# A hybrid encoder block in 3 x fp32r products on one core: rooms, ties and early weights in the input projection; keys, last-used tiles and sums of w_out in the tail

## The chip, the core and the metric

The kernel runs on one core of a Trainium2 chip. The core has a matrix engine (TensorE, PE in the profile), a vector engine (VectorE, DVE), a scalar engine (ScalarE, ACT), a general engine (GpSimd, POOL) and a queue that issues transfers (SyncE, SP). Each works through its own list of instructions in order; semaphores make one wait for another. The metric is the device time of one execution in microseconds (us), and lower is better.

## The reference

For x of 2048 tokens by 1024 channels, all in fp32:

```python
h = rms_norm(x, norm_pre_g)
u_a, z_a, q, k, v, o, z_b, gates, g_a, g_b = split(h @ w_in)          # 9 x 1024 columns and 16 gates
pooled = multiscale_pool(u_a)                                         # windows 2, 4, 8, 16, mean minus token
y_a = (pooled @ pool_mix_w (per group)) * pool_scale * silu(z_a)
q, k = silu(conv5([q, k]))                                            # centred, per channel
h_fwd, h_bwd = mlstm(q, k, v, gates) in both directions               # 4 heads of 256, chunks of 128
y_b = headwise_rms(h_fwd + h_bwd) * mlstm_norm_g * sigmoid(o) * silu(z_b)
merged = sigmoid(g_a + b0) * (y_a @ w_proj_pool) + sigmoid(g_b + b1) * (y_b @ w_proj_mlstm)
out = x + rms_norm(merged @ w_out, norm_post_g)
```

One direction of mlstm carries a 256 x 256 state per head from chunk to chunk. Per chunk it adds keys, weighted by exponentials of the gates, times values, and reads the state with the queries.

## The kernel before

Every large product is made of three fp32r matmuls: each operand is split into an upper half, a copy by ACT (L98), and a lower half, the difference, by DVE or POOL (L102); PE adds upper x upper, upper x lower and lower x upper (L110 to L112 or L1038 to L1040).

**Input projection (`phase1`, 0 to about 1494 us).** 36 pairs of column blocks are run over each half of 1024 tokens. `operands` loads x, computes the row norms (`sums`, with two dummy matmuls `busy` at L281) and makes the sums S1 to S4 (`combos`, L210 to L217) of Strassen's scheme. The first two pairs are plain products; the others take seven block products in place of eight (`strassen`). There ACT copies the first bank (p1, L463) and DVE adds it to later banks (u2 at L469, u3 at L474, output sums at L685 through `collect`); the next product into a bank waits until these have read it. In the first half `prep_w` makes each pair's weight sums T1 to T4 (L426) and `keep_w` stores them; in the second half `again_w` loads them. The gates' product leaves PSUM by an ACT copy (gsb, L671), for which the products of `fold` (fps, L373) wait; they multiply pool_mix_w into the weights of u. In the second half 16 pieces of w_proj_pool are fetched, split and stored again (`split_ahead`, one per pair from pair 12, 2 tiles from the pool `wt` of 3), and 32 masks for mlstm are built in tiles of the same pool (`masked`). Halo columns of neighbouring tokens are copied into each raw tile (L703, L765) before the convolution or the pooling.

**mLSTM (`mlstm`, to about 1830 us).** A backward pass over head 0's chunks 15 to 1 comes first: `back1` transposes keys (L1277, ACT copies them at L1280), `keys` weighs them (kw on ACT at L1239, upper half on DVE at L1240, lower half on POOL at L1241), `back2` updates the state. Then 64 steps, one per head and chunk, run the forward pass and the outputs (`front1` to `front3`, `finish`), with the next head's backward pass beside them. The pool `io` holds everything that rotates here, the gate tile gb and the normalised outputs too. The last yb store (L1470) is the last thing of this stage on SP.

**Projections and output.** `branch_a` multiplies y_a by w_proj_pool (paps, 8 groups of 128 columns x 4 blocks of 512 tokens) and by its gate (L1182), to about 1992 us; `branch_b` does y_b (pb), to about 2174; `output` is again Strassen's scheme, its weight sums of w_out made by `out_weights` (differences L1081) in part during `branch_b`, in part at its own start. The pools `w1` (8 tiles of 4 KB a partition), `w1b` (4) and `w2` (16) hold split weights. `w1` is opened at the start of the tail, and first written when weights of w_proj_pool are loaded during the steps (`turns`).

**What sets the order.** A scheduler places the instructions of each engine, by priority and by times that it simulates; `issue_after` ties one instruction behind another on the same engine only, and waits for data come besides. All DMAs are issued by SP in one list, so a transfer that has to wait for its data or for room holds up all that come after it. A tile's memory is free for the next tile when its last reader has ended; for a stored tile that is the landing of its store.

## Time and profile before

| | us |
|---|---|
| median of 3 runs | 2350.88 |
| lowest to highest | 2348.56 to 2352.04 |
| the profiled execution, own time | 2351.66 |
| its span in the trace | 2349.9 |
| PE busy | 2291.2 |
| DVE, POOL, ACT busy | 1428.9, 1182.4, 884.2 |
| mean granted clock of PE | 0.994 |
| moved by DMA | 550.80 MB |

The span is the time from the first to the last instruction of the profiled execution; the execution's own time lies 1.76 us above it. Times in the views count from the start of the span. In a row of a timeline stand the start, the length, the engine, the line, the operation, output and input, their shapes and, in brackets, how long the engine had been idle before it and what ended that. Lines (L...) are those of the kernel before.

### The profile page before, as it was taken

What the parts mean: (1) busy time and instruction counts of PE and PEld (TensorE: products, weight loads), DVE (VectorE), ACT (ScalarE), POOL (GpSimd) and SP (SyncE); (2) the same over time, 40 slices, a digit from 0 to 9 for tenths busy, and PEclk for the clock granted to TensorE, in tenths of its full rate; (3) what the DMA queues carried; (4) which work ended last, traced back from release to release, by engine and by line L of the source; (5) the groups of instructions that cost most, each with busy time, mean ns of one, the idle gap of its engine ahead of it and who ended that gap; (6) DMA issues with size and microseconds to landing.
All of it is one profiled execution on the core that took longest, in us unless ns stands there. A gap on an engine that the chain in (4) does not pass through costs nothing.

```text
span 2349.9 us, 32919 instructions
## 1 busy us (share of the span) xinstructions
PE 2291.2 (98%) x11545; PEld 1938.3 (82%) x11545; DVE 1428.9 (61%) x2383; ACT 884.2 (38%) x1795; POOL 1182.4 (50%) x917
## 2 busy tenths in 40 slices
PE   7999999999999999999989999999999899999998
PEld 5788888888888788888878788799998688999776
DVE  7765656767765565546656665489886322454765
ACT  5434332433334423322322233477676201111432
POOL 4655555666654534456555555355556200234865
PEclk9999999999999999999999999999999999999999
DMA  5567766766675366788888787777676745687753
GB/s 210 188 245 266 261 218 233 258 233 223 225 281 206 111 215 204 227 295 290 288 295 297 263 296 252 271 242 243 225 219 195 244 141 166 228 269 272 264 191 126
DMA packets 229238, 550.80 MB, mean 234 GB/s; under 512 B 23120, under 2 KB 70352, under 8 KB 229072
## 3 DMA queue, kind: packets, MB, share of 16 engines
q1 hardware_dynamic: 229072, 548.69, 68.2%
q8 instruction: 91, 1.49, 0.3%
q14 instruction: 75, 0.61, 0.1%
HBM read 335.22 MB, written 213.39 MB: 233 GB/s over the span
## 4 chain that ended last, share of the span: by engine, by line
PE 81%; DMA 7%; DVE 6%; issue 2%; POOL 2%; ACT 1%; SPq 1%; DVEq 0%; POOLq 0%; ACTq 0%
PE bankB L110 7%; PE bankB L112 7%; PE bankB L111 7%; PE bankA L110 5%; PE bankA L111 5%; PE bankA L112 5%; PE bankC L110 5%; PE bankC L111 5%; PE bankC L112 5%; PE num L1367 4%; PE pb L1040 3%; PE pb L1038 3%; PE pb L1039 3%; PE paps L1038 2%; PE paps L1039 2%; PE paps L1040 2%
## 5 line engine op out<-in xcount | busy, mean ns | idle before, releaser
L102 POOL TENSOR_TENSOR wB<-wraw,wB 128x512 fp32r<-128x512 f32 x224 | 338.0, 1513 | 302.1 <-ACT wB L98 214.5
L98 ACT ACTIVATE wB<-wraw 128x512 fp32r<-128x512 f32 x228 | 141.8, 625 | 271.8 <-PE bankB L112 133.7
L102 POOL TENSOR_TENSOR wT<-wt,wT 128x512 fp32r<-128x512 f32 x102 | 148.9, 1464 | 132.7 <-ACT wT L98 105.9
L718 DVE SCALAR_TENSOR_TENSOR acc<-raw,conv_w,acc 128x1026 f32<-128x1026 f32 (+1 forms) x96 | 152.2, 1597 | 10.5 <-ACT acc L713 9.7
L1040 PE MATMUL pb<-oxs,w_proj_mlstm 128*128 128x256 f32 x512 | 143.9, 281 | 0.0
L1039 PE MATMUL pb<-oxs,w_proj_mlstm 128*128 128x256 f32 x512 | 143.8, 281 | 0.0
L1038 PE MATMUL pb<-oxs,w_proj_mlstm 128*128 128x256 f32 x512 | 143.8, 281 | 0.0
L98 ACT ACTIVATE wT<-wt 128x512 fp32r<-128x512 f32 x136 | 85.2, 629 | 150.1 <-PE bankB L112 57.1
L1351 POOL TENSOR_TENSOR qs<-q,isc 128x256 f32<-128x256 f32 x120 | 89.8, 752 | 85.3 <-PE num L1367 53.9
L110 PE MATMUL bankB<-S3h,wT 128*128 128x512 f32 x272 | 106.7, 392 | 3.7 <-DVE u L469 3.7
L110 PE MATMUL bankB<-A22h,wT 128*128 128x512 f32 x272 | 106.3, 391 | 2.9 <-DVE u L474 2.9
L1038 PE MATMUL paps<-pys,w_proj_pool 128*128 128x512 f32 x256 | 102.0, 399 | 6.2 <-DMA w_proj_pool<-wp 3.8
L110 PE MATMUL bankA<-A12h,wB 128*128 128x512 f32 x272 | 107.9, 397 | 0.0
L110 PE MATMUL bankC<-S4h,wB 128*128 128x512 f32 x272 | 106.2, 391 | 1.2 <-DVE raw L685 1.2
L111 PE MATMUL bankB<-S2l,wT 128*128 128x512 f32 x272 | 106.6, 392 | 0.0
L112 PE MATMUL bankB<-S2h,wT 128*128 128x512 f32 x272 | 106.0, 390 | 0.7 <-DVE wT L102 0.7
L112 PE MATMUL bankB<-S3h,wT 128*128 128x512 f32 x272 | 106.6, 392 | 0.0
L111 PE MATMUL bankB<-S3l,wT 128*128 128x512 f32 x272 | 106.6, 392 | 0.0
L110 PE MATMUL bankC<-S1h,wT 128*128 128x512 f32 x272 | 106.5, 392 | 0.0
L111 PE MATMUL bankC<-S4l,wB 128*128 128x512 f32 x272 | 106.4, 391 | 0.0
L110 PE MATMUL bankA<-A11h,wB 128*128 128x512 f32 x272 | 106.2, 390 | 0.0
L112 PE MATMUL bankA<-A12h,wB 128*128 128x512 f32 x272 | 106.1, 390 | 0.0
(413 smaller groups left out, 7063.6 us busy)
## 6 DMA issues: line engine op xcount, KB each, us to landing
wt<-wT SPq DMA_DIRECT2D x136, 512.0 KB, 4.6
wT<-wt SPq DMA_DIRECT2D x136, 512.0 KB, 5.9
wraw<-in_w_in SPq DMA_DIRECT2D x98, 512.0 KB, 5.2
vh<-vnh SPq DMA_DIRECT2D x16, 516.0 KB, 3.9
vl<-vnl SPq DMA_DIRECT2D x16, 516.0 KB, 5.9
v<-vh SPq DMA_DIRECT2D x16, 516.0 KB, 8.8
v<-vl SPq DMA_DIRECT2D x16, 516.0 KB, 8.2
xT<-in_xT SPq DMA_DIRECT2D x16, 512.0 KB, 6.3
```

The costliest lines, as they stand in the source:

```text
L98: self.upper = nc.scalar.activation(hi, x, AF.Copy)
L102: return eng.tensor_tensor(lo, x, hi.bitcast(F32), op=ALU.subtract)
L110: nc.tensor.matmul(ps, wh, xh, start=start and kt == 0, stop=False, skip_group_check=True)
L111: nc.tensor.matmul(ps, wh, xl, start=False, stop=False, skip_group_check=True)
L112: end = nc.tensor.matmul(ps, wl, xh, start=False, stop=stop and kt == 3, skip_group_check=True)
L718: nc.vector.scalar_tensor_tensor(acc[:, :n], raw[:, tap : tap + n], self.cw[:, ct, tap : tap + 1], acc[:, :n], op0=ALU.mult, op1=ALU.add,)
L1038: nc.tensor.matmul(ps, wh, xh, start=i == 0, stop=False)
L1039: nc.tensor.matmul(ps, wh, xl, start=False, stop=False)
L1040: nc.tensor.matmul(ps, wl, xh, start=False, stop=i == n)
L1351: nc.gpsimd.tensor_tensor(qs[d], q[:, :, ck], isc[:, d, j % 2, None, :].to_broadcast([P, 2, P]), op=ALU.mult)
L1367: nc.tensor.matmul(pn, qs[d][:, kt, :], state[:, kt, :], start=kt == 0, stop=False)
```

## The change

Eight edits, of which none removes a product:

- Start-up: the first dummy matmul is tied behind the row sums' matmuls, the second is issued twice.
- First half: the lower half of S1 is made by DVE (by POOL in the second half as before); two of the input tiles exchange rooms between the pools; pair 3's weight preparation is tied behind an evacuation of the plain pairs and behind the gates' copy.
- Second half: `split_ahead` becomes `fetch_ahead` (tiles and load, where it stood) and `split_ahead` (split and stores, after the pair's third step, tied behind p1's copy and behind the last read bank). Halo copies and constant columns are tied behind the last collected sum.
- First backward pass: kw and both halves of the key take tiles of `w1`, two per key, in place of `io`'s; a one-element Exp is put behind chunk 8's kw.
- The tiles used last in mlstm (gb, h, ssq, h1, r) move from `io` to a new pool `last` under it.
- The remaining pool weights are loaded before the last yb store; the weights of w_proj_mlstm are tied behind the second gate load of `branch_a`; the pool `xp` has two tiles in place of three.
- `sums_ahead`, four times in `branch_a`, makes T1, T3, T4 and B22 of w_out, split, and stores them.
- `made_weights` loads these in place of making them in `out_weights`.

```diff
@@ -203,7 +203,7 @@
-    def combos(self, H, j, a11, a12, a21, a22):
+    def combos(self, H, j, a11, a12, a21, a22, le):
@@ -211,7 +211,7 @@
-        self.put(H, "S1", j, s1, "act", "pool")
+        self.put(H, "S1", j, s1, "act", le)
@@ -224,7 +224,7 @@
-        for b, q, where in ((0, 0, "raw"), (0, 2, "acc"), (0, 1, "acc"), (0, 3, "acc"), (1, 0, "raw"), (1, 2, "raw"), (1, 1, wc), (1, 3, wc)):
+        for b, q, where in ((0, 0, "raw"), (0, 2, "acc"), (0, 1, "acc"), (0, 3, "acc"), (1, 0, "raw"), (1, 1, "raw"), (1, 2, wc), (1, 3, wc)):
@@ -255,12 +255,16 @@
-                nc.tensor.matmul(ps[:, i : i + 1], acc[:, i * P : (i + 1) * P], self.one_c, start=True, stop=True)
-            busy(X[7][0][:, :P], X[7][0])
+                done = nc.tensor.matmul(
+                    ps[:, i : i + 1], acc[:, i * P : (i + 1) * P], self.one_c, start=True, stop=True
+                )
+            with tc.issue_after(done.ins):
+                busy(X[7][0][:, :P], X[7][0])
...
-            busy(self.rstd[:, :1].to_broadcast([P, P]), X[7][0])
+            for _ in range(2):
+                busy(self.rstd[:, :1].to_broadcast([P, P]), X[7][0])
@@ -320,7 +324,7 @@
-        ends = [self.combos(H, j, X[j][0], X[4 + j][0], X[j][1], X[4 + j][1]) for j in range(4)]
+        ends = [self.combos(H, j, X[j][0], X[4 + j][0], X[j][1], X[4 + j][1], ("dve", "pool")[half]) for j in range(4)]
@@ -460,7 +464,7 @@
-        nc.scalar.activation(p1, bank["A"], AF.Copy)
+        self.first_copy = nc.scalar.activation(p1, bank["A"], AF.Copy)
@@ -600,7 +604,10 @@
-                            with tc.issue_after(self.scaled[8].ins) if i == 2 else ExitStack():
+                            ties = [self.scaled[8]] if i == 2 else [self.evac, self.gated] if i == 3 else []
+                            with ExitStack() as behind:
+                                for t in ties:
+                                    behind.enter_context(tc.issue_after(t.ins))
@@ -613,7 +620,7 @@
-                            self.split_ahead(*divmod(i - PRE, KT))
+                            held = self.fetch_ahead(*divmod(i - PRE, KT))
@@ -628,6 +635,8 @@
+                    if half == 1 and PRE <= i < PRE + 2 * KT:
+                        self.split_ahead(*held)
@@ -668,7 +677,7 @@
-            nc.scalar.activation(g, ps, AF.Copy)
+            self.gated = nc.scalar.activation(g, ps, AF.Copy)
@@ -682,7 +691,8 @@
-            return nc.vector.tensor_tensor(d, ps, add, op=ALU.add)
+            self.collected = nc.vector.tensor_tensor(d, ps, add, op=ALU.add)
+            return self.collected
@@ -702,8 +712,9 @@
-                nc.vector.tensor_copy(raw[:, 0:4], self.halo_qk[:, ct, :])
-                nc.vector.memset(raw[:, HALF + 4 : HALF + 6], 0.0)
+                with self.tc.issue_after(self.collected.ins):
+                    nc.vector.tensor_copy(raw[:, 0:4], self.halo_qk[:, ct, :])
+                    nc.vector.memset(raw[:, HALF + 4 : HALF + 6], 0.0)
@@ -734,8 +745,9 @@
-            nc.vector.memset(hi[:, :, DH:].bitcast(F32), 1.0)
-            nc.vector.memset(lo[:, :, DH:].bitcast(F32), 0.0)
+            with self.tc.issue_after(self.collected.ins) if half else ExitStack():
+                nc.vector.memset(hi[:, :, DH:].bitcast(F32), 1.0)
+                nc.vector.memset(lo[:, :, DH:].bitcast(F32), 0.0)
@@ -762,8 +774,9 @@
-                nc.vector.tensor_copy(raw[:, 0:16], self.halo_u[:, ct, :])
-                nc.vector.memset(raw[:, HALF + 16 : HALF + 24], 0.0)
+                with self.tc.issue_after(self.collected.ins):
+                    nc.vector.tensor_copy(raw[:, 0:16], self.halo_u[:, ct, :])
+                    nc.vector.memset(raw[:, HALF + 16 : HALF + 24], 0.0)
@@ -888,6 +901,8 @@
+        for n in ("T1", "T3", "T4", "B22"):
+            sp[f"wo{n}"] = self.dram(f"wo{n}", [P, 4, 2, 512])
@@ -1001,12 +1016,18 @@
-    def split_ahead(self, e, kt):
+    def fetch_ahead(self, e, kt):
...
-        self.split(hi.bitcast(F32R), x.bitcast(F32R), x, "act", "dve")
+        return e, kt, x, hi
...
+    def split_ahead(self, e, kt, x, hi):
...
+        nc, tc = self.nc, self.tc
+        with tc.issue_after(self.first_copy.ins), tc.issue_after(self.read_banks[-1].ins):
+            self.split(hi.bitcast(F32R), x.bitcast(F32R), x, "act", "dve")
@@ -1056,7 +1077,32 @@
-            self.nc.sync.dma_start(t.bitcast(F32), self.sp["wp"][:, kt, e])
+            i = self.nc.sync.dma_start(t.bitcast(F32), self.sp["wp"][:, kt, e])
+        return i
...
+    def sums_ahead(self, j, pool):
...
+        nc = self.nc
+        t = [pool.tile([P, 2, 512], F32, tag="ws", name=self.nm("ws")) for _ in range(4)]
+        for i, (k, e) in enumerate(((0, 0), (0, 1), (1, 0), (1, 1))):
+            nc.sync.dma_start(t[i][:, 1], self.a["w_out"][:, 4 * k + j, e * 512 : (e + 1) * 512])
+        b11, b12, b21, b22 = (x[:, 1] for x in t)
+        sub = lambda d, x, y: nc.vector.tensor_tensor(d, x, y, op=ALU.subtract)
+        t1, t3, t4, t2 = b11, b12, b21, t[3][:, 0]
+        sub(t1, b12, b11)
+        sub(t3, b22, b12)
+        sub(t2, b22, t1)
+        sub(t4, b21, t2)
+        for i, n in enumerate(("T1", "T3", "T4", "B22")):
+            hi, x = t[i][:, 0], t[i][:, 1]
+            self.split(hi.bitcast(F32R), x.bitcast(F32R), x, "act", "pool" if i % 2 else "dve")
+            nc.sync.dma_start(self.sp[f"wo{n}"][:, j], t[i])
...
+    def made_weights(self, W, n):
+        for j in range(4):
+            t = next(self.rooms).tile([P, 2, 512], F32R, tag="w", name=self.nm(f"w{n}"))
+            self.nc.sync.dma_start(t.bitcast(F32), self.sp[f"wo{n}"][:, j])
+            W.setdefault(n, []).append((t[:, 0], t[:, 1]))
@@ -1080,14 +1126,8 @@
-        if "T3" in names:
-            diff("T1", b[1], b[0], 0)
-            diff("T3", b[3], b[1], 1)
-        else:
-            diff("T1", b[1], b[0], 1)
-            diff("T2", b[3], b[1], 0 if "T4" in names else 1)
-        if "T4" in names:
-            diff("T4", b[2], b[0], 1)
+        diff("T1", b[1], b[0], 1)
+        diff("T2", b[3], b[1], 1)
@@ -1156,10 +1196,11 @@
-    def branch_a(self, W, X):
+    def branch_a(self, W, X, pool):
...
-        room = [("x", None)] * 3 + [("kT", i) for i in self.free["kT"]]
+        sums = list(range(4))
+        room = [("x", None)] * 2 + [("kT", i) for i in self.free["kT"]]
@@ -1170,7 +1211,9 @@
-                    nc.sync.dma_start(s, sp[f"sga{d // 2}"][:, :, cut])
+                    load = nc.sync.dma_start(s, sp[f"sga{d // 2}"][:, :, cut])
+                    if t == 0 and d == 2:
+                        self.gates_in = load
@@ -1185,6 +1228,8 @@
+                if t > 0 and (d == 6 or t == 2 and d == 1):
+                    self.sums_ahead(sums.pop(0), pool)
@@ -1198,6 +1243,7 @@
+            last = es.enter_context(tc.tile_pool(name="last", bufs=2, reuse_waits="tile"))
@@ -1232,14 +1278,21 @@
-                out = split2(io, [P, DH], f"k{d}", bufs=KB)
...
-                    kw = io.tile([P, DH], F32, tag="kw", name=self.nm("kw"))
-                    nc.scalar.activation(kw, kn[h, c // 4][:, c % 4, :], AF.Copy, scale=col["w"][:, ix(d, h, c)])
+                    kw = self.w1.tile([P, 2, 512], F32, tag="w", name=self.nm("kw"))[:, 0, :DH]
+                    k = self.w1.tile([P, 2, 512], F32R, tag="w", name=self.nm("k"))
+                    out = k[:, 0, :DH], k[:, 1, :DH]
+                    up = nc.scalar.activation(kw, kn[h, c // 4][:, c % 4, :], AF.Copy, scale=col["w"][:, ix(d, h, c)])
...
+                    if c == NC_ // 2:
...
+                        none = last.tile([P, 1], F32, tag="none", name="none", bufs=1)
+                        with tc.issue_after(up.ins):
+                            nc.scalar.activation(none, self.one_c, AF.Exp)
...
+                out = split2(io, [P, DH], f"k{d}", bufs=KB)
@@ -1301,7 +1354,7 @@
-                gb = cur["gb", h, g] = io.tile([P, 2, 512], F32, tag="gb", name=self.nm("gb"))
+                gb = cur["gb", h, g] = last.tile([P, 2, 512], F32, tag="gb", name=self.nm("gb"))
@@ -1383,13 +1436,13 @@
-                    cur["h"] = io.tile([P, 4, DH], F32, tag="h", name=self.nm("h"))
-                    cur["ssq"] = io.tile([P, 4], F32, tag="ssq", name=self.nm("ssq"))
+                    cur["h"] = last.tile([P, 4, DH], F32, tag="h", name=self.nm("h"))
+                    cur["ssq"] = last.tile([P, 4], F32, tag="ssq", name=self.nm("ssq"))
...
-                h1 = io.tile([P, DH], F32, tag="h1", name=self.nm("h1"))
+                h1 = last.tile([P, DH], F32, tag="h1", name=self.nm("h1"))
...
-                    r = io.tile([P, 1], F32, tag="r", name=self.nm("r"), bufs=4)
+                    r = last.tile([P, 1], F32, tag="r", name=self.nm("r"), bufs=4)
@@ -1466,8 +1519,7 @@
-            while made:
-                nc.sync.dma_start(*made.pop(0))
+            return made
@@ -1509,10 +1561,10 @@
-                    for j in range(4):
-                        self.out_weights(WO, j, ("T1", "T3"))
-        for j in range(4):
-            self.out_weights(WO, j, ("T4", "B22"))
+                    for k in ("T1", "T3"):
+                        self.made_weights(WO, k)
+        for k in ("T4", "B22"):
+            self.made_weights(WO, k)
@@ -1631,7 +1683,7 @@
-            w1 = es.enter_context(tc.tile_pool(name="w1", bufs=8, side="right", reuse_waits="tile"))
+            w1 = self.w1 = es.enter_context(tc.tile_pool(name="w1", bufs=8, side="right", reuse_waits="tile"))
@@ -1647,16 +1699,20 @@
-            self.mlstm(turns, ends)
+            made = self.mlstm(turns, ends)
...
-            self.xp = es.enter_context(tc.tile_pool(name="xp", bufs=3, reuse_waits="tile"))
+            self.xp = es.enter_context(tc.tile_pool(name="xp", bufs=2, reuse_waits="tile"))
...
-            self.pool_weights(WA, 1, range(4, 8), w2)
-            self.branch_a(WA, ya)
-            WB = self.weights("w_proj_mlstm", 0, range(8), raws, w2)
-            WB.update(self.weights("w_proj_mlstm", 1, range(4), raws, w2))
-            WB.update(self.weights("w_proj_mlstm", 1, range(4, 8), raws, w1))
+            with tc.issue_after(self.pool_weights(WA, 1, range(4, 8), w2).ins):
+                for out in made:
+                    tc.nc.sync.dma_start(*out)
+            with tc.tile_pool(name="ws", bufs=4, reuse_waits="tile") as ws:
+                self.branch_a(WA, ya, ws)
+            with tc.issue_after(self.gates_in.ins):
+                WB = self.weights("w_proj_mlstm", 0, range(8), raws, w2)
+                WB.update(self.weights("w_proj_mlstm", 1, range(4), raws, w2))
+                WB.update(self.weights("w_proj_mlstm", 1, range(4, 8), raws, w1))
```

## The prediction

> **What bounds the kernel now.** I read the page's busy times first, then the windows by stage, then what TensorE (PE) waited for, then the granted clock behind those waits.
>
> ```profile
> span 2349.9 us, 32919 instructions
> PE 2291.2 (98%) x11545; PEld 1938.3 (82%) x11545; DVE 1428.9 (61%) x2383; ACT 884.2 (38%) x1795; POOL 1182.4 (50%) x917
> ```
>
> PE is busy 98% of the span. The change takes no product away, so its prize lies in the 58.7 us in which PE stands (2349.9 - 2291.2) and in what standing does to its clock. Where does it stand? Columns of the next view: the window, its length, then busy time of PE, PE's weight loads, VectorE (DVE), ScalarE (ACT) and GpSimd (POOL), PE's granted clock, the DMA engines' busy share, GB/s.
>
> ```profile
> 0.00:130.00 130.00, 111.86 (x459) 87.20 (x460) 92.81 (x134) 63.16 (x114) 73.06 (x50) 0.97 0.56 203
> 130.00:1130.00 1000.00, 996.32 (x4463) 822.82 (x4462) 606.33 (x769) 361.89 (x617) 540.79 (x343) 1.00 0.68 237
> 1130.00:1490.00 360.00, 350.69 (x1537) 288.63 (x1536) 209.98 (x230) 111.72 (x169) 184.34 (x120) 0.99 0.79 268
> 1490.00:1522.00 32.00, 28.82 (x180) 23.66 (x179) 22.06 (x55) 20.66 (x53) 15.12 (x21) 1.00 0.94 359
> 1830.00:1850.00 20.00, 13.83 (x53) 9.78 (x52) 7.85 (x10) 2.31 (x4) 3.00 (x2) 0.94 0.85 293
> 2174.00:2246.00 72.00, 66.12 (x268) 51.66 (x267) 52.80 (x61) 30.16 (x63) 54.39 (x42) 0.95 0.75 259
> 2246.00:2350.00 104.00, 94.92 (x409) 76.22 (x407) 64.92 (x86) 34.31 (x78) 62.55 (x52) 0.98 0.44 148
> ```
>
> Idle PE per stage is length minus PE busy: start-up 18.1 us, the long first stretch 3.7, the second half's later pairs 9.3, the first backward pass 3.2, the start of the pooling projection 6.2, the start of the output product 5.9, the end 9.1 (most of it after the last matmul).
>
> ```profile
> PE busy L281 <- DMA xT<-in_xT: 9.2, 1, 9.2
> PE bankB L110 <- DVE u L474: 5.9, 5, 2.2
> PE bankB L110 <- DVE u L469: 5.8, 4, 2.3
> PE vtr L744 <- DVE raw L685: 5.2, 3, 4.0
> PE fps L373 <- ACT gsb L671: 5.1, 1, 5.1
> PE paps L1038 <- DMA w_proj_pool<-wp: 3.8, 4, 1.6
> PE paps L1038 <- DVE sga L1182: 2.4, 1, 2.4
> PE rbp L183 <- POOL rstd L161: 1.7, 1, 1.7
> ```
>
> (total, times, longest.) The first one is the input arriving and isn't touched. Each of the others is named by an edit below. The clock adds to them:
>
> ```profile
> 86.20:92.90 6.70, 4.98 (x12) 3.97 (x13) 3.15 (x5) 3.84 (x9) 4.53 (x3) 0.50 1.02 357
> 1328.60:1332.00 3.40, 3.40 (x10) 2.66 (x9) 3.06 (x3) 1.45 (x3) 0.00 (x0) 0.50 0.83 257
> 2240.00:2243.30 3.30, 3.30 (x10) 2.53 (x9) 0.04 (x1) 3.30 (x9) 2.62 (x3) 0.50 0.95 296
> ```
>
> Behind a long stand the clock is 0.50 for some 3.4 us or twice that. In the undisturbed stretch a matmul takes 0.223 us (996.32 / 4463), so 3.4 us would hold 15; here there are 10, both ends counted whole. I price such a window at 1.5 us, and the double one at 2.3 (4.98 busy less 12 x 0.223).
>
> **The change part by part.**
>
> *Start-up* (L281). One dummy matmul moves behind the row sums into the 1.7 us wait for rstd; the second is doubled. They may end some 0.6 us later than the first real product wants, or bring the full clock one window of 1.5 earlier. Between -1 and +2; I take +1.
>
> *First half's sums and pair 3.* The lower half of S1 goes from POOL to DVE, input tiles change rooms, and pair 3's weight preparation is held behind the gates' copy out of PSUM (L671).
>
> ```profile
> 56.10 6.88 DVE L211 TENSOR_TENSOR xT<-xT,xT 128x512 f32<-128x512 f32 x4
> 68.61 1.28 DVE L217 TENSOR_TENSOR xT<-xT,xT 128x512 f32<-128x512 f32 x2
> ```
> ```profile
> 54.01 6.72 POOL L102 TENSOR_TENSOR S1l<-xT,S1h 128x512 fp32r<-128x512 f32 x4 [3.70 <-ACT S1h L98]
> ```
> ```profile
> 84.22 0.79 DVE L426 TENSOR_TENSOR wt<-wraw,wt 128x512 f32<-128x512 f32 x1 [2.10 <-DMA wraw<-in_w_in]
> ```
> ```profile
> 85.11 0.63 ACT L98 ACTIVATE wT<-wt 128x512 fp32r<-128x512 f32 x1 [1.94 <-DVE wt L426]
> ...
> 87.30 0.57 ACT L671 ACTIVATE gsb<-gps 32x512 f32<-32x512 f32 x1
> ```
>
> DVE's four subtractions take 1.7 us each while POOL runs S1's lower halves, and 0.64 each when POOL is silent. Four lower halves on DVE at 0.64 cost 2.6 and free some 4 us of slowed DVE work: DVE gains about 1.6 and POOL's next group starts 6.7 earlier. The 5.1 us stand at L373 waits for ACT's copy (L671), behind a weight copy that waits for DVE, which waits 2.10 for a load. Putting that weight work behind L671 takes it off this chain. It is late then by the same few us for pair 3, whose first use is over a pair (some 20 us) away. Prize: 5.1, 0.7 just before it, 2.3 of clock = 8.1. I take +7, bounds 3 to 8.1 (the load may still be late for pair 2).
>
> *Second half: split-ahead in two steps, late ties.* Sixteen pieces of w_proj_pool are fetched, split and stored beside the pairs. Today the split stands in ACT's order as soon as the load is issued; what ACT sat idle for before its 16 copies (us, times):
>
> ```profile
>   DMA wp<-in_w_proj_pool: 35.1, 7
>   DMA nm<-nm: 24.7, 5
> ```
> ```profile
> 1226.07 1.22 DVE L765 COPY raw<-halo_u 128x16 f32<-128x16 f32 x1 [1.96 <-POOL acc L723]
> ```
>
> ACT stood 5 us on average (59.8 in 12) before a split, and DVE, which makes the lower half, behind it; u (L469, L474), on which the next product's bank waits, stood behind that. The 4.0 at L744 comes from the same order: a halo copy that waited 1.96 for POOL stood ahead of the sum that PE needed. With the fetch before the pair and the split after its first product the load has landed, and with the halo ties behind the collected sum that copy no longer precedes it. Prize: 9.3 idle plus two clock windows (behind the 4.0 and the 2.3), 12.3. I take +9, bounds 3 to 12.3, since the split's own 2 x 0.6 us still falls near the sums.
>
> *First pass: keys four deep in w1, table loaded early.* Fifteen keys get four buffers in place of two. The stretch 1490-1522 has 3.2 us idle and DMA at 0.94, so hardly more than 1.5 is to be had. But where do the new buffers lie? w1's eight slots were first written long after the first stage; now the first key writes them at its end, and by the memory layout they overlap the first stage's last tiles, one of them the last gate tile.
>
> ```profile
> 1498.22 0.51 ACT L1239 ACTIVATE kw<-kn,col_w 128x256 f32<-128x256 f32 x1 [0.40 <-POOL k L1241]
> ```
> ```profile
> 1501.79 0.32 SPq L843 DMA_DIRECT2D sga<-u  x1
> ```
> ```profile
> sga<-u SPq DMA_DIRECT2D x1, 256.0 KB, 9.0
> ```
>
> That tile's store is issued at 1501.79 and lands 9.0 later, at 1510.8. The key that gets its slot is one of the first three; the third's copy ran at 1498.22. It must wait 12.6 us on ACT, and behind it ACT's transposed copies, so PE runs dry. Less the 1.5 gained, plus a clock window or two: I take -13; bounds -16 and, if the store goes earlier or another tile is there, +1.5.
>
> *Stage two's end: last-used tiles apart, pool weights ahead of the last store.*
>
> ```profile
> SPq L1470 <- DVE gb L1421: 17.0, 1, 17.0
> SPq L1059 <- DMA yb<-gb: 2.0, 1, 2.0
> ```
>
> The queue that issues every DMA stood 17.0 us at the last yb store; four weight loads and three gate loads stood behind it. With the loads first, and their room no longer shared with tiles used last, they land before PE asks. The yb store is read again only in the next projection, over 150 us later. Prize: 6.2 idle plus one clock window, 7.7. I take +6.5, bounds 2 (loads still compete) to 7.7. xp's lost buffer costs nothing: gate tiles rotate over the free kT tiles too.
>
> *Four of w_out's sums made ahead.* In the pooling projection, 4 times: 4 loads, 4 DVE subtractions, 4 splits (4 ACT, 2 DVE, 2 POOL), 4 stores; later 16 loads replace the differences and splits at the start of the output product. There PE stands 5.9 us and gets two slow windows (8.9) because DVE makes weights while sums wait:
>
> ```profile
> L1081 DVE TENSOR_TENSOR wo<-wraw,wo x9: 674/1108/1774, 2174.6 to 2200.7; 128x512 f32<-128x512 f32 x9
> L1081 DVE TENSOR_TENSOR wo<-wo x4: 694/1488/1784, 2179.2 to 2190.8; 128x512 f32<-128x512 f32 x4
> ```
>
> Of these 13 differences (shortest, median, longest ns) nearly all go, 16 us of DVE, and the splits of T4 and B22 with them. The added sums (in all 16 subtractions and 8 lower halves on DVE, some 1.2 us each, 29 us) lie in a stage in which PE never stands and DVE works a quarter of the time:
>
> ```profile
> 1850.00:1995.00 145.00, 145.00 (x637) 118.15 (x637) 35.52 (x46) 20.02 (x35) 20.18 (x15) 1.00 0.57 182
> ```
>
> They cost nothing there under this cover (-3 if a gate product on DVE comes late behind them). But 8 MB come back by DMA: at the 357 GB/s of the row above 8 of the 16 loads take 11.7 us, just before T4 is wanted. I take +5.5, bounds -3 and 8.9.
>
> Sum: 1 + 7 + 9 + 6.5 + 5.5 = 29, less 13 = **16 us**. The profiled execution took 2351.66 (span 2349.9 and 1.76 around it), 0.8 over the median 2350.88, so 16 off gives 2335.7, or 2335 against the median.
>
> A rule speaks against part of this. The row: 0.50 for 3.4 us followed stands of only 2.2 to 2.4 us. The Trainium skill, page "TensorE: Matmul & The Clock Gate", section "HAM oscillation — how this bites in real kernels", says that idle gaps matter to the clock only above about 3.4 us. By it, four of my clock windows (one in the second half, one at the pooling projection, two in the output) would not be the gaps' doing and would stay: 6 us less, 2341. The rows disagree with it here, so the sum keeps them.
>
> **The rivals.**
>
> *No stall in the first pass.* The same sum with +1.5 in place of -13: 30.5 off, **2320**. For it: the last gate store could be issued earlier, since something now waits for it, and ACT can be given other work meanwhile. Against: 12.6 us between two rows, and SP is in order.
>
> *Slower: the wait moves to the wt rooms.* A piece holds two of three wt slots from before its pair to its landed store, over a pair's length, and the 32 masked tiles share them. The next fetch then stands on SP for a free slot, and the kept weights' loads stand behind it. It decides once the stand exceeds what those loads are ahead, which I estimate at 8 us, from a landing of 5.9 in a pair of some 20 (84 matmuls in most pairs; 1537 in 350.69 us):
>
> ```profile
> wT<-wt SPq DMA_DIRECT2D x136, 512.0 KB, 5.9
> ```
>
> A stand of 10 costs 2 us in each of 16 pairs, 32 us. The other parts gain 20: net -10.5 without the first pass's stall, -25 with it, 2361 to 2376; middle **2368**. Against: fetches come just once in a pair, and 20 us is long.
>
> *The change trades waits.* Each stand is replaced by another at the next late thing (pair 3's weights at pair 3, pool weights behind gates, loaded sums behind DMA). Half of 29 less 13 leaves 1.5: **2349**. For it: DMA share is 0.75 to 0.94 in the stages touched.
>
> **How the numbers follow.** Chances: forecast 0.44 (own range 2328 to 2343), no stall 0.30 (2313 to 2327), slower 0.12 (2358 to 2378), trade 0.14 (2343 to 2354). The range 2315 to 2352 leaves out the slower case, and 0.07 at the ends of the others. About 0.2% (4.7 us) is what a measurement of this kernel can tell from no change. Faster: 0.44 + 0.30 + 0.03 = 0.77; same 0.11, all from the trade; slower 0.12.
>
> **What would show it.** Start-up: no stand at L373 and clock 1.00 at 86-93. Second half: ACT's waits for w_proj_pool loads near zero, PE idle from 1130 on below 3 us. First pass: a key's ACT copy waiting for the store of the gate tile some 10 us, the pass ending near 1530 in old time. At 1830 PE idle below 1.5 us; at 2174-2246 below 3 us. Wrong, if the first key waits for nothing of the kind, or if SP stands at the fetches of w_proj_pool for more than 8 us a pair.

## The result and the profile after

The changed kernel takes 2371.93 us (median of 6 runs, 2368.1 to 2374.41) against 2350.73 for the kernel before: **0.92% slower**, ratio 1.0092 with a 95% interval of 1.0080 to 1.0104. Forecast were 2335 and a range of 2315 to 2352. The range does not hold it. Two executions of kernels below (3270.61 and 3503.92 us) ran in a slower state at a lower granted clock, and all times and ratios are of the others.

First the busy times, then the windows, set to the same work as those of before (shifted by how late that work is); columns as before.

```profile
span 2369.2 us, 32982 instructions
PE 2292.6 (97%) x11547; PEld 1940.6 (82%) x11547; DVE 1410.6 (60%) x2383; ACT 883.6 (37%) x1796; POOL 1180.8 (50%) x913
```
```profile
0.00:130.00 130.00, 112.23 (x473) 88.28 (x474) 90.41 (x140) 62.88 (x115) 75.79 (x47) 0.97 0.58 208
130.00:1107.00 977.00, 975.13 (x4370) 805.24 (x4369) 588.22 (x745) 351.92 (x600) 516.40 (x329) 1.00 0.67 231
1107.00:1519.00 412.00, 381.60 (x1636) 310.92 (x1635) 220.87 (x253) 120.22 (x187) 208.10 (x132) 0.97 0.78 262
1519.00:1555.00 36.00, 24.06 (x136) 18.97 (x135) 18.53 (x47) 21.34 (x55) 15.35 (x21) 0.81 0.97 344
1867.00:1887.00 20.00, 20.00 (x92) 16.40 (x91) 11.06 (x14) 4.39 (x8) 3.88 (x3) 1.00 0.79 259
2203.00:2276.00 73.00, 73.00 (x321) 59.33 (x320) 35.42 (x48) 28.06 (x58) 47.84 (x39) 1.00 0.82 294
```

PE is busy for about the same time (2292.6 against 2291.2) and stands 18 us longer. The two late stages are mended: PE never stands in the 20 us at the start of the pooling projection (6.2 before) nor in the 73 us at the start of the output product (5.9 before). The loss is in two places: the second half's later pairs (30.4 idle in 412) and the first backward pass (11.9 idle in 36, clock 0.81). What PE waited for (total, times, longest):

```profile
PE bankB L110 <- DVE u L478: 20.1, 10, 10.6
PE bankB L110 <- DVE u L473: 12.0, 3, 5.4
PE ssqp L258 <- DVE sq L254: 11.8, 1, 11.8
PE kt L1330 <- DMA kT<-kT: 5.3, 3, 2.3
PE vtr L756 <- DVE vnl L102: 4.6, 1, 4.6
```

u2 is now L473 and u3 L478. The first stand of the kernel has another name only because the first dummy moved. To give every part its own sum, the table takes the same TensorE instruction in both traces.

| PE reaches | before, us | after, us | after is late by | part | gave | forecast |
|---|---|---|---|---|---|---|
| first product of pair 2 | 74.20 | 72.76 | -1.44 | start-up | +1.4 | +1 |
| first product of pair 3 | 100.38 | 97.67 | -2.71 | S1's half, rooms, pair 3 | +1.3 | +7 |
| a pair of the second half at 1107 | 1111.28 | 1106.71 | -4.57 | late ties (below) | +1.9 | |
| first product of the last pair | 1468.69 | 1493.44 | +24.75 | split-ahead and late ties | -29.3 | +9 |
| first paps product | 1792.71 | 1830.10 | +37.39 | keys in w1 | -12.6 | -13 |
| end of the last paps | 1992.66 | 2021.01 | +28.35 | last-used tiles, order of loads | +9.0 | +6.5 |
| end of the last pb | 2174.27 | 2203.97 | +29.70 | sums ahead: their cost | -1.4 | +5.5 |
| end of the last matmul | 2341.70 | 2361.10 | +19.40 | sums ahead: their gain | +10.3 | (with it) |

No run takes the parts of the last three rows apart. From the first to the last paps product it takes 197.9 to 200.0 us in the three kernels without them (before, two-step split alone, late ties alone) and 190.9 to 191.0 in the others.

### The profile page after: what moved, and what is told of

The parts are those of the page before. It is cut to its first block, busy times and chain, and to the rows that moved or that the text cites. A ratio compares the mean times of both kernels' runs of the same rounds, so it can differ in the third digit from the quotient of the medians.

```text
span 2369.2 us, 32982 instructions
## 1 busy us (share of the span) xinstructions
PE 2292.6 (97%) x11547; PEld 1940.6 (82%) x11547; DVE 1410.6 (60%) x2383; ACT 883.6 (37%) x1796; POOL 1180.8 (50%) x913
## 4 chain that ended last, share of the span: by engine, by line
PE 78%; DMA 10%; DVE 5%; issue 2%; POOL 2%; ACT 1%; SPq 1%; DVEq 0%; POOLq 0%; ACTq 0%
PE bankB L110 7%; PE bankB L111 7%; PE bankB L112 7%; PE bankA L110 5%; PE bankA L112 5%; PE bankA L111 5%; PE bankC L110 5%; PE bankC L111 5%; PE bankC L112 5%; PE num L1420 4%; PE pb L1059 2%; PE pb L1060 2%; PE pb L1061 2%; DVE acc L729 2%; PE cu L1059 1%
## 5 line engine op out<-in xcount | busy, mean ns | idle before, releaser
L1044 POOL TENSOR_TENSOR nm<-nm,mask 128x256 f32<-128x256 f32 x64 | 63.1, 996 | 174.0 <-DMA nm<-negM 146.0
L110 PE MATMUL bankB<-A22h,wT 128*128 128x512 f32 x272 | 108.6, 399 | 19.3 <-DVE u L478 19.3
L473 DVE TENSOR_TENSOR u<-bankB,p 128x512 f32<-128x512 f32 x76 | 52.1, 685 | 100.9 <-PE bankB L112 93.8
L430 DVE TENSOR_TENSOR wt<-wraw,wt 128x512 f32<-128x512 f32 x68 | 63.5, 934 | 76.4 <-POOL wT L102 57.5
L111 PE MATMUL bankB<-A22l,wT 128*128 128x512 f32 x272 | 107.6, 396 | 0.0
L110 PE MATMUL bankA<-A12h,wB 128*128 128x512 f32 x272 | 107.6, 395 | 0.0
L112 PE MATMUL bankB<-A22h,wT 128*128 128x512 f32 x272 | 107.4, 395 | 0.0
```

Source lines behind the costliest of these rows:

```text
L110: nc.tensor.matmul(ps, wh, xh, start=start and kt == 0, stop=False, skip_group_check=True)
L111: nc.tensor.matmul(ps, wh, xl, start=False, stop=False, skip_group_check=True)
L112: end = nc.tensor.matmul(ps, wl, xh, start=False, stop=stop and kt == 3, skip_group_check=True)
L430: nc.vector.tensor_tensor(t, x, y, op=ALU.subtract)
```

## The experiments

Each kernel was timed beside the kernel before; the ratio is to that, with its 95% interval. No kernel leaves out or changes what is computed; one moves the masks in time.

### Split-ahead in one step

```diff
-                            held = self.fetch_ahead(*divmod(i - PRE, KT))
+                            self.split_ahead(*self.fetch_ahead(*divmod(i - PRE, KT)))
...
-                    if half == 1 and PRE <= i < PRE + 2 * KT:
-                        self.split_ahead(*held)
...
-        with tc.issue_after(self.first_copy.ins), tc.issue_after(self.read_banks[-1].ins):
-            self.split(hi.bitcast(F32R), x.bitcast(F32R), x, "act", "dve")
+        self.split(hi.bitcast(F32R), x.bitcast(F32R), x, "act", "dve")
```

> The changed kernel with split-ahead in one step again (fetch, split and stores where they stood before, no tie); all else stays. Between pair 50 of the second half's neighbourhood and the projection's end the changed kernel lost 27.6 us against the kernel before (4.6 ahead at its pair at 1107, 24.7 behind at its last pair). Theory W, the two-step split is what lost it: the projection's end comes back by some 26 to 32, the time is 2340 to 2346. Theory T, the late ties of halo copies and constants lost it: the time stays at 2366 to 2374.

Measured: 2346.5 us, 0.9992 (0.9983 to 1.0002). 25 us come back, and the last pair starts 0.8 us ahead of the kernel before. Theory W.

### The late ties taken away

```diff
-                with self.tc.issue_after(self.collected.ins):
+                with ExitStack():
```

(the same for the constant columns)

> The changed kernel without the ties of halo copies and constant columns behind the collected sum; the two-step split stays. Theory W (the two-step split lost the 27.6 us): the time stays within 6 us of 2372, PE still stands 10 us at a time before the product that waits for u. Theory T (the late ties): 2340 to 2348.

Measured: 2373.42 us, 1.0111 (1.0095 to 1.0128). Nothing comes back; as long as the two-step split is there, the ties decide nothing.

### The two-step split alone, on the kernel before

(the kernel before with `fetch_ahead`, `split_ahead` and their two calls as in the changed kernel)

> The kernel before with nothing but the two-step split-ahead. Theory W: 20 to 32 us slower than before, 2371 to 2383. Theory T: within 5 us of before. A third possibility, that the two-step split only hurts together with the ties: 0 to 10 us slower.

Measured: 2381.45 us, 1.0146 (1.0131 to 1.0161). The two-step split costs 33 us by itself; in its trace the last pair starts 27.9 later than before. PE waits for u as in the changed kernel:

```profile
PE bankB L110 <- DVE u L474: 19.9, 5, 7.1
PE bankB L110 <- DVE u L469: 10.1, 4, 6.5
```

**How it costs that.** The fetch has kept its place in the program; only the split went back. But in the kernel before the 16 fetches were issued 20.4 us (median) ahead of the first product of their pair, and in the changed kernel 6.3 us behind it. There the queue SP issued one piece's fetch at 1163.83. That is 17.6 us after the first product of the pair (1146.22) whose split was to use it. The fetch before it was issued at 1139.86, and ACT had by then been standing for it since 1130.8:

```profile
1139.86 0.54 SPq L1023 DMA_DIRECT2D wp<-in_w_proj_pool  x1
...
1159.29 0.32 SPq L1047 DMA_DIRECT2D nm<-nm  x1
1163.83 0.33 SPq L1023 DMA_DIRECT2D wp<-in_w_proj_pool  x1
```
```profile
1147.99 0.63 ACT L98 ACTIVATE wp<-wp 128x512 fp32r<-128x512 f32 x1 [17.23 <-DMA wp<-in_w_proj_pool]
```

What SP itself waited for, from pair 10 on (a mask is nm, a piece wp):

```profile
SPq L1047 <- DMA nm<-negM: 59.4, 25, 4.8
SPq L1047 <- POOL nm L1044: 33.9, 30, 2.4
SPq L1040 <- DMA wp<-wp: 26.8, 9, 4.7
...
SPq L1023 <- DMA nm<-nm: 17.9, 8, 4.1
```

It is a ring through three rooms. A mask's load (L1040) waits for the room of a piece, until that piece's store has landed; its store (L1047) waits for the load and for POOL's addition; the next fetch (L1023) waits for the room of a mask, until that store has landed. The tie makes the ring slow: DVE's lower half, tied behind the last read bank, comes 14.7 us (median) after ACT's copy, 0.7 in the kernel before. For the piece copied at 1147.99 it is this row:

```profile
1159.19 0.68 DVE L102 TENSOR_TENSOR wp<-wp,wp 128x512 fp32r<-128x512 f32 x1
```

From the issue of a fetch to the landing of the piece's last store, until which its rooms are taken, it is 29.9 us (median), before 14.3, and a pair takes some 20.

The longest stand of PE, 10.6, comes of both. ACT stood 6.2 before its next split, and a convolution's sigmoid (L733) and product (L734) came behind that:

```profile
1166.69 0.63 ACT L98 ACTIVATE wp<-wp 128x512 fp32r<-128x512 f32 x1 [6.21 <-DMA wp<-in_w_proj_pool]
1167.23 2.00 ACT L733 ACTIVATE raw<-acc 128x1026 f32<-128x1026 f32 x2
```
```profile
1168.35 4.78 POOL L734 TENSOR_TENSOR acc<-acc,raw 128x1026 f32<-128x1026 f32 x2 [5.11 <-ACT raw L733]
```

The first of the two products was done at 1170.8. SP, which issues everything in one list, stood for a mask's room until 1172.3 and issued this product's store (qT<-acc) at 1173.75; it landed at 1181.8. Only then ACT got its tile and DVE its sum:

```profile
1181.92 1.24 ACT L724 ACTIVATE acc<-late,conv_b,conv_w 128x1022 f32<-128x1022 f32 x1 [11.13 <-DMA qT<-acc]
```
```profile
1183.19 3.58 DVE L729 SCALAR_TENSOR_TENSOR acc<-late,conv_w,acc 128x1022 f32<-128x1022 f32 x2 [9.51 <-ACT acc L724]
1186.69 0.68 DVE L478 TENSOR_TENSOR u<-bankB,p 128x512 f32<-128x512 f32 x1
```

u stands behind that, and PE behind u: the 10.6.

### Rooms or ties: two runs

Masks moved to pairs 28 to 34:

```diff
-                            for u in range(max(0, 8 * (i - 10) // 6), max(0, min(32, 8 * (i - 9) // 6))):
+                            for u in range(*((i - 10, i - 9) if 10 <= i < 12 else (2 + 30 * (i - 28) // 7, 2 + 30 * (i - 27) // 7) if 28 <= i < 35 else (0, 0))):
```

(22 masks leave pairs 12 to 27, not the 29 that the expectation names; with the 8 that were there before, 30 now stand in pairs 28 to 34.)

> The changed kernel with 29 of the 32 masked tiles moved from beside pairs 12 to 27 to pairs 28 to 34, so that the three rooms they share with the pieces of w_proj_pool are the pieces' own meanwhile; two-step split and ties as changed. Theory R (the piece holds two of three rooms until the split, the masks' loads, additions and stores go through the third, and each next fetch waits for one of them): ACT's 75.5 us of waits for fetched pieces fall below 25, and 15 to 28 us come back, 2344 to 2357. Theory P (the split's tied place in ACT's and DVE's order is what makes u late, whatever the room): less than 6 us come back, 2366 to 2374.

The split after the third step, without its two ties:

```diff
-        with tc.issue_after(self.first_copy.ins), tc.issue_after(self.read_banks[-1].ins):
-            self.split(hi.bitcast(F32R), x.bitcast(F32R), x, "act", "dve")
+        self.split(hi.bitcast(F32R), x.bitcast(F32R), x, "act", "dve")
```

> The changed kernel with the split still made after the pair's third step but without the two ties behind p1's copy and behind the last read bank. Theory R (rooms held too long): the time stays at 2364 to 2376, since the piece is still split late in the scheduler's list, or falls by part. Theory P (the ties' place): 15 to 28 us come back, 2344 to 2357.

Measured: 2347.48 us, 0.9988 (0.9979 to 0.9998), and 2348.5 us, 0.9989 (0.9980 to 0.9999). Each gives some 24 us back; the theories were not alternatives.

Without the two ties the scheduler puts ACT's copies where the one-step kernel has them (first and last at 995.2 and 1302.4; with one step at 996.3 and 1303.7). DVE's half comes 0.7 us after the copy, the piece's rooms are taken for 15.0 (medians), and the fetches are issued 20.0 ahead of their pair, with all masks in the ring. So this run in effect undoes the two-step split, and it shows that the ring alone does not make the fetch late: the tie does, by keeping the rooms taken. Nor is it the sum of ACT's stands that costs. Before its 16 copies ACT stood 102.0 in this run and 83.7 in the changed kernel; most of the 102.0 is this:

```profile
  DMA wp<-in_w_proj_pool: 56.0, 8
  DMA nm<-nm: 40.6, 5
```

The difference is in what stands behind. DVE waits for the convolutions' first step on ACT, and its u come behind that; these waits from 1000 to 1500 were, first in the changed kernel, then in this run:

```profile
DVE acc L729 <- ACT acc L724: 40.3, 11, 11.2
```
```profile
DVE acc L729 <- ACT acc L724: 15.5, 10, 3.3
```

With the masks moved and the ties kept ACT never stands for a fetched piece; all that it stood before its 16 copies was this:

```profile
L98 ACT ACTIVATE wp<-wp x16: 622/623/633, 1013.3 to 1302.5; 128x512 fp32r<-128x512 f32 x16
its engine sat idle before it (us, times) until:
  DVE wp L102: 1.3, 1
```

Its fetches were issued 9 to 25 us ahead of their pair. Between the pairs at 1107 and 1337 PE did not stand once for 0.4 us, and against the kernel before it gained 12.9 us there. That is the size of the prize of 12.3 in the prediction, but this run also takes the masks' work out of that stretch, so it does not show that the split alone would earn it. From the pair at 1337 to the last, the moved masks took it back: 19.6 us were lost.

### The upper half's tile taken at the split

```diff
-        x, hi = (self.wt_pool.tile([P, 512], F32, tag="wt", name=self.nm("wp")) for _ in range(2))
+        x = self.wt_pool.tile([P, 512], F32, tag="wt", name=self.nm("wp"))
...
+        hi = self.wt_pool.tile([P, 512], F32, tag="wt", name=self.nm("wp"))
```

(the second in `split_ahead`)

> The changed kernel in which the tile for a piece's upper half is taken at the split and not at the fetch, so that a piece holds one of the three rooms while it waits and not two; split and ties as changed. Theory R (rooms): the masks have two rooms, the next fetch is issued earlier, ACT's 75.5 us of waits for fetched pieces at least halve, and 12 to 28 us come back, 2344 to 2360. Theory R2 (one room too few for the masks is not it; the fetch needs its room a whole pair ahead): less than 6 us, 2366 to 2374.

> The same with the first pass's keys in the old rotating pool. If theory R holds and the two-step split then brings what was forecast for it (12.3 us of stands and slow clock between pairs 12 and 27, of which the run with the masks moved shows 12.9 gained up to pair 27), the time is 2320 to 2328, below the 2334.6 of the kernel with one step. If the shared rooms still cost part of it, 2330 to 2345.

Measured: 2370.52 us, 1.0101 (1.0076 to 1.0126), and with the keys' old room 2359.71 us, 1.0054 (1.0036 to 1.0071). A miss: ACT still stood 83.3 us for fetched pieces. One room less during the wait does not help: from the fetch to the landing of the last store it is 29.7 us (median), against 29.9 in the changed kernel.

### The first pass

Keys in the rotating pool again:

```diff
-                    kw = self.w1.tile([P, 2, 512], F32, tag="w", name=self.nm("kw"))[:, 0, :DH]
-                    k = self.w1.tile([P, 2, 512], F32R, tag="w", name=self.nm("k"))
-                    out = k[:, 0, :DH], k[:, 1, :DH]
+                    out = split2(io, [P, DH], f"k{d}", bufs=KB)
+                    kw = io.tile([P, DH], F32, tag="kw", name=self.nm("kw"))
```

> The changed kernel with the first pass's keys back in the rotating pool of mlstm, two deep; the table preload stays (its one element in another tile). In the changed kernel the first state product came 16.1 us after the first transpose of keys, before 3.0 us, and 12.7 us were lost by the end of this stage. Theory S (the keys' new room waits for the last gate tile's store): 12 to 15 us come back, the time is 2357 to 2361. Rival Q (the pass is late because its loads of keys and values are late in the transfer queue, whatever the room): at most 4 us come back, 2367 to 2372.

Measured: 2359.29 us, 1.0049 (1.0034 to 1.0065): 12.6 back, theory S. From the first transpose to the first paps product it took 298.8 us, before 298.4, in the changed kernel 311.1. So the early table load, which this run keeps, is worth nothing that shows.

How the wait looks in the changed kernel:

```profile
1526.73 0.32 SPq L856 DMA_DIRECT2D sga<-u  x1
```
```profile
1530.89 0.91 ACT L1263 ACTIVATE k<-kn,col_w 128x256 fp32r<-128x256 f32 x2
1533.39 0.38 ACT L1333 ACTIVATE kn<-kt 128x256 f32<-128x256 f32 x1 [1.59 <-PE kt L1330]
...
1534.22 0.89 ACT L1286 ACTIVATE kw<-kn,col_w 128x256 f32<-128x256 f32 x2
1535.85 1.31 ACT L1286 ACTIVATE kw<-kn,col_w 128x256 f32<-128x256 f32 x3 [0.74 <-DMA sga<-u]
```

The store is issued at 1526.73 and lands 9.0 later, at 1535.7; the third key starts with it. On ACT the wait shows as 0.74 only, since in its list the transposed copies stand ahead of the keys; PE stood for transposes and loads instead (5.3 for kT) and had its first state product at 1535.16, 16.1 after its first transpose (3.0 before).

The last gate's tile elsewhere, and the first five keys elsewhere:

```diff
-        u2 = pool.tile([P, n], F32, tag="p", name=self.nm("u2"))
+        u2 = pool.tile([P, n], F32, tag="raw" if self.edge and not swap and self.half else "p", name=self.nm("u2"))
```

> The changed kernel in which one tile of the second half's last pair, the one that holds the last gate and whose store lands last (issued 1526.7, landed 1535.8), lies in another pool, so that no room of w1 is under it. The store before it was issued at 1519.6. Theory S (the keys wait for that landing): the first state product comes 6 to 9 us earlier against the first transpose, 6 to 10 us come back, 2362 to 2366. Otherwise (the scheduler's order alone, or another store): at most 2 us, 2369 to 2374.

```diff
+                    if c > 10:
+                        out = split2(io, [P, DH], f"k{d}", bufs=KB)
+                        kw = io.tile([P, DH], F32, tag="kw", name=self.nm("kw"))
+                    else:
```

(the lines of the changed kernel follow, indented)

> The changed kernel in which the first five keys of the first pass take the old rotating rooms and only the other ten take rooms of w1, the first of them some 7 to 8 us later. Theory S (only the landing of the last gate tile's store matters): w1's third key is then wanted near the landing, 9 to 13 us come back, 2358 to 2363. If the whole of w1 is late by other tiles' stores or by the order that the scheduler makes of it, at most 5 us, 2366 to 2372.

Measured: 2367.4 us, 1.0090 (1.0068 to 1.0112), and 2366.6 us, 1.0073 (1.0054 to 1.0093). With u elsewhere the first key starts at 1527.92, right after the landing of the store before it (issued 1518.71, 9.0 to landing):

```profile
1527.92 0.50 ACT L1286 ACTIVATE kw<-kn,col_w 128x256 f32<-128x256 f32 x1
```

The first state product comes 10.6 after the first transpose, 5.5 earlier. Of the 12.6 this gives back 4.5 by the medians, 2.4 by the traces (308.6 us from the first transpose to the first paps product) and 1.1 against the kernel before timed beside each: a miss, since 6 to 10 were expected. The landing of that other store fits the rest, but no run moves it. Five keys elsewhere brought 5.3 by the medians, of 9 to 13. Their profile is that of the execution of 3503.92 us, so why the other ten still came late is open; in its order they stand in one batch behind the transposes, as in the changed kernel.

### Both undone, and the late ties again

The edits of split-ahead in one step and of the keys' old room together; then also the late ties taken away:

> The changed kernel with both losing parts undone: split-ahead in one step, keys in the rotating pool. If the two losses add (25.3 by the run with one step, 12.6 by the run with the keys' old room), the time is 2332 to 2336, 0.6% faster than before. If they overlap (an earlier projection makes the last gate store's wait shorter or longer), it differs from that by over 4 us.

Measured: 2334.61 us, 0.9933 (0.9917 to 0.9948). The two losses add.

> The kernel with split-ahead in one step and keys in the rotating pool (2334.6), and besides without the ties of halo copies and constant columns behind the collected sum. If these ties are worth what was forecast (the stand of 4.0 before the value transposes and its slow window, 5.5), the time is 2338 to 2342. If they bring nothing, 2333 to 2337.

Measured: 2328.45 us, 0.9917 (0.9892 to 0.9942); run again it gave 2330.72 (below). The ties rather cost than gain. Alone on the kernel before:

> The kernel before with nothing but the ties of halo copies and constant columns behind the collected sum. As forecast (the stand of 4.0 before the value transposes goes): 3 to 6 us faster than before. Rival (the tied copies only come late for the convolutions, and other sums stand instead): same within 3 us, or 3 to 8 us slower.

Measured: 2355.74 us, 1.0028 (1.0016 to 1.0039): 6.8 us slower. In its trace 2.9 of them are lost by the last pair; the rest is in stages that the ties do not touch. The stand of 4.0 before the value transposes does go, but others come:

```profile
PE bankB L110 <- DVE u L469: 6.8, 6, 2.4
PE bankB L110 <- DVE u L474: 4.1, 3, 2.2
```

(pairs from 1107 on; before it was 3.7 and 1.7 there, and the 4.0). In the earlier pairs the ties remove two stands that the kernel of this section without ties still has (1.17 at 859, 1.19 at 968), as the kernel before has them (1.17 at 863, 0.74 at 972); that is the +1.9 of the table.

### The first half

```diff
-        self.put(H, "S3", j, s3, "act", "pool")
+        self.put(H, "S3", j, s3, "act", le)
```

> The kernel with split-ahead in one step, keys in the rotating pool and no late ties, and besides the lower half of S3 made by the vector engine in the first half, as S1's is. Theory G (GpSimd bounds the weights of pair 2: its four S3 halves took 16.0 us beside the vector engine, and that engine then stood 7.4 for GpSimd): the stand of 5.4 at 84 and its slow clock go, 5 to 9 us less than e17. Rival D (pair 2's weights are bounded by their loads or by ACT): within 2 us of e17.

The edit undone (S1's half on POOL, rooms as before, pair 3 untied):

> The kernel of e17 with the first half's edit undone (S1's lower half on GpSimd, the rooms of x as before, pair 3's weights not tied). By the traces of before and of the changed kernel it should be 1 to 2 us slower than e17; by the prediction's term 7 us slower.

> Split-ahead in one step, keys in the rotating pool, no late ties: the same kernel as the fastest so far, as the base for this call. 2325 to 2332, 0.7 to 0.95% faster than before.

Measured: 2326.47 us, 0.9905 (0.9891 to 0.9918); 2331.51, 0.9929 (0.9916 to 0.9941); 2330.72, 0.9925 (0.9910 to 0.9939). In the times the first half's edit makes no difference that shows. The traces show a small one: from the first product of pair 2 to that of pair 3 it takes 25.9 to 26.7 us in the four kernels without the edit and 24.4 to 25.7 in twelve with it (S3's halves still on POOL). Why it is not more is in the trace of the changed kernel:

```profile
55.13 16.02 POOL L102 TENSOR_TENSOR S3l<-xT,S3h 128x512 fp32r<-128x512 f32 x4 [6.27 <-ACT S3h L98]
```
```profile
73.69 1.75 DVE L430 TENSOR_TENSOR wt<-wraw,wt 128x512 f32<-128x512 f32 x1 [7.42 <-POOL wT L102]
```

DVE was done early (66.3), then stood 7.42 for POOL. The first row covers four lower halves, which did not take the same time: the first took 12.29, until 1.15 after DVE's last operation, and the other three 1.3 each:

```profile
55.13 12.29 POOL L102 TENSOR_TENSOR S3l<-xT,S3h 128x512 fp32r<-128x512 f32 x1 [6.27 <-ACT S3h L98]
```
```profile
67.39 3.77 POOL L102 TENSOR_TENSOR S3l<-xT,S3h 128x512 fp32r<-128x512 f32 x3
```

The edit is not what brings this about. In the run with the late ties alone, whose first half is that of the kernel before, the first operation of S1's lower halves on POOL was drawn out in the same way (the row below), while in the kernel before POOL and DVE took turns at 1.7 each. Which of the two ways comes is not explained by any run here.

```profile
52.26 11.25 POOL L102 TENSOR_TENSOR S1l<-xT,S1h 128x512 fp32r<-128x512 f32 x1 [3.70 <-ACT S1h L98]
```

The stand at fps went, and one of 5.4 for u2 came. With S3's halves on DVE too, that stand is 2.95, and pair 3's first product comes 1.8 us earlier against the kernel before than in the run beside it. Theory G is right in sign; of its 5 to 9 us that place gives 1.8. The 4.2 between the medians holds another 3 from pairs in the second half, and they are no gain that shows: the traces of the two runs of the kernel beside it (one step, old keys, no late ties) differ there by 2.7. The kernel with S3's halves on DVE is the fastest: 0.95% faster than the kernel before.

## Why the prediction was wrong, point by point

- **Start-up**: +1.4 for +1. The size fits, but the spread is as large: the three traces with the old start-up reach that product at 74.20, 73.25 and 72.47, fourteen with the new one at 71.58 to 72.76.
- **First half**: +1.3 for +7. The step "DVE gains about 1.6 and POOL's next group starts 6.7 earlier" failed in its second half: POOL's next group started 5.6 earlier (55.13, before 60.69) but took 16.0 in place of 6.8, since its first operation lasted 12.3 beside DVE, and ended 3.6 later. Both prices, 1.7 and 0.64, were read from rows in which the two engines took turns or POOL was silent; the third case, one POOL operation drawn out to the end of DVE's run, was not among them.
- **Split-ahead**: -27.4 over both rows of the table for +9, the cause of the miss. The step that failed is "With the fetch before the pair and the split after its first product the load has landed". The fetch kept its place in the program, but in time it went from 20.4 us ahead of its pair's first product to 6.3 us behind it (medians, at most 17.6), because the later split keeps a piece's rooms taken for 29.9 us in place of 14.3. The bounds (3 to 12.3) held no loss at all, although the rival beside them described one. The sign set for it, SP standing more than 8 us a pair at the fetches, did not come (17.9 in 8 waits, the longest 4.1): SP stood at the masks' loads and stores of the same ring.
- **The slower rival** had the place right (rooms held over a pair's length, SP standing). Its time, 2368, and its price of 32 us (33 in the run with the two-step split alone) came out near the measured ones by luck, for its path was wrong: not the kept weights' loads came late (0.2 us in all), but ACT's tied split, the convolutions' stores, and u behind both. And its chance of 0.12 was far too low. "fetches come just once in a pair, and 20 us is long" left out that one or two masks go through the same three rooms in that pair (22 in 16 pairs).
- **Late ties**, part of the same term: forecast with the 4.0 they would remove; they remove it and lose 2.9 by the last pair (6.8 in the medians), by new stands for u.
- **First pass**: -12.6 for -13. The place is right: with the keys' old room the loss goes. The size is in part luck, for the 12.6 us wait that it was worked out from is that of one store, and with that store's tile elsewhere only 1 to 4.5 come back. The wait came out as PE's stands for transposes and keys rather than as a block on ACT.
- **Pooling projection**: +9.0 for +6.5, and **sums ahead**: +8.9 for +5.5, their cost 1.4 at the first pb. Both mechanisms fit the traces (SP still stands 15.3 us at the last yb store, 17.0 before, but with the weight loads ahead of it), both sizes were too small: all stands and all slow windows of these stages went.
- **The clock**: the Trainium skill, page "TensorE: Matmul & The Clock Gate", section "HAM oscillation — how this bites in real kernels", tells to keep PE's idle gaps below about 3.4 us. By that rule the prediction had four windows that would have stayed. The three in the two mended stages went with their stands of 2.2 to 2.4 us (granted clock 1.00 in both), so the trace disagrees with the rule; the fourth lies where new stands came, and tells nothing.

## What to carry to other kernels

A step that is moved back holds its rooms longer, and the next transfer, at the same place in the program, comes later: draw the ring of tiles that share the pool, work out how long each tile is taken, and ask of each wait in the ring which queue it holds up. A tie is a promise that what it orders is never late; put together with a late transfer it moves the lateness to everything behind it. And tiles in memory that another stage has just left start no earlier than the stores from that memory land, so look at what lies under a new buffer before making it deeper.

## What the runs showed of the hardware

- POOL and DVE subtracting 128x512 tiles at the same time come out in two ways. In the kernel before they took turns, 1.7 us each (0.6 and 1.3 alone). In the changed kernel DVE kept 0.6 to 0.7 each over 18 operations without a pause, and one POOL operation lasted 12.29, until 1.15 after the last of them ended. In the fastest kernel one lasted 7.58, again until 1.15 after DVE's last:

```profile
61.53 7.58 POOL L102 TENSOR_TENSOR wB<-wraw,wB 128x512 fp32r<-128x512 f32 x1 [13.38 <-ACT wB L98]
```

- The length of a stand alone does not tell whether the clock halves. A stand of 2.04 us was followed by a slow window, one of 2.46 at the same place in another run was not. The granted clock in the traces shows why: it changes at times that lie whole multiples of 3.413 us apart (in the kernel before it fell to 0.50 at 1229.61, 1328.60, 1847.42, 2188.76 and 2239.96, which are 29, 152, 100 and 15 of them). Cut into these windows, the first stand lies whole in one, in which PE is busy 1.38; the second, from 225.63 to 228.09, lies across a border, and PE is busy 2.48 and 1.88 in its two:

```profile
222.53:225.94 3.41, 1.38 (x7) 0.80 (x6) 3.38 (x4) 0.59 (x1) 0.98 (x1) 1.00 0.79 263
225.94:229.35 3.41, 3.41 (x8) 2.73 (x9) 2.03 (x2) 2.99 (x6) 2.87 (x2) 0.50 0.11 44
```
```profile
223.15:226.56 3.41, 2.48 (x11) 1.71 (x10) 2.23 (x3) 0.00 (x0) 2.54 (x2) 1.00 0.38 153
226.56:229.97 3.41, 1.88 (x8) 1.58 (x9) 2.16 (x3) 2.44 (x4) 1.31 (x1) 1.00 0.51 155
229.97:233.38 3.41, 3.41 (x17) 2.81 (x16) 1.49 (x1) 1.77 (x4) 3.41 (x3) 1.00 0.38 153
```

The first is the run with S3's halves on DVE, the second the one beside it, both at the stand for u3. In 17 of the 18 traces (all but that of 3503.92 us), each of the 78 windows at full clock in which PE stood 1.9 us or more was followed by one at 0.50, and none of those in which it stood less than 1.55 (from 30 to 2330 us; in between both occur). The Trainium skill, page "TensorE: Matmul & The Clock Gate", section "What's actually happening", tells of a free-running window of about 3.4 us. The traces agree with that.
